# Where the taps of a 31-tap convolution are put in VectorE's queue

## The chip, the cores and the metric

The kernel runs on one core of one Trainium2 chip. The time is that of the device for one execution, in microseconds (us). TensorE (PE) multiplies, VectorE (DVE), ScalarE (ACT) and GpSimd (POOL) work elementwise, SyncE (SP) issues most loads. Every engine runs its own queue in the order in which the program was built, and waits for the others by semaphores.

## The reference

One layer of an encoder on x of 1024 positions by 1024 channels, all in float32. Cut to the part that matters:

```python
h = rms_norm(x, norm_mix_g[l]) * (1.0 + sc1) + sh1
proj = jnp.einsum('bsd,de->bse', h, w_in[l])                 # 1024 -> 7 * 1024
b_s, c_s, v_s, v_c, gl_c, gate_br = jnp.split(proj, SPLITS[:-1], axis=-1)
y_a = b_s * causal_dwconv(c_s * v_s, conv_short_w[l])        # 3 taps
y_a = jnp.einsum('bsc,cd->bsd', y_a, w_short_out[l])
u = v_c * jax.nn.sigmoid(gl_c)
u = causal_dwconv(u, conv_conf_w[l]) + conv_conf_b[l]        # 31 taps
u = jax.nn.silu(layer_norm(u, conf_ln_g[l], conf_ln_b[l]))
y_b = jnp.einsum('bsc,cd->bsd', u, w_conf_out[l])
g_a, g_b = jnp.split(jax.nn.sigmoid(gate_br), 2, axis=-1)
mix = jnp.einsum('bsd,de->bse', g_a * y_a + g_b * y_b, w_o[l])
```

After it come a residual, a SwiGLU feed-forward layer with its own residual, and a last RMSNorm.

## The kernel before

Channels lie on the 128 partitions (`KC` = 8 blocks), positions along the free axis in two halves of `H` = 512. Float32 products are made of three matmuls: an operand is split into a high and a low part (`wh`, `wl` for weights: ACT casts `wh`, L214, and POOL subtracts to `wl`, L215; `th`, `tl` for activations), and high*high, high*low and low*high are summed in PSUM (`mm3`, L309, L310, L312).

The input projection's 56 column blocks are made after a short lead in 12 *duals* (`PAIRS`). A dual takes two pairs of column blocks and replaces eight block products by seven, in the manner of Strassen and Winograd. The products are named by `PRODUCTS = "1265734"` and run in that order, each in two halves, one for each pair (p = 0, 1). A half is 12 matmuls into one PSUM bank. Banks are added up in place: 1, 6, 7 and 4 all go to bank x of their pair, 2 to bank y, 5 and 3 to bank z. So 7 may start only when the sum of 6 has been read out of x, and 4 only when that of 7 has. POOL also makes the sums of weight blocks that the products need (L234, L236, L238, L255).

`win_evac` reads the banks. After 1, 6 and 5 ACT copies them out (L642, L657). After 2, 7 and 3 DVE reads them with one addition, `plus` (L602), and each such instruction is appended to the list `reads`: six in a dual, in the order 2p0, 2p1, 7p0, 7p1, 3p0, 3p1. After 4, kinds "u" and "g" take a sigmoid on ACT (L670), "p" and "q" a product on DVE (`minus_times`, L606). Kind "u" makes an input of the 31-tap convolution (`u[j]`, L648, L672), "p" that of the 3-tap convolution (`short_conv`, first ACT L593, then DVE L595), "q" multiplies its result (L652), "g" two gates, whose sigmoids (L654, L664) wait in the list `late` until the next copy of ACT.

The 31-tap convolutions of the eight blocks, `conv(j)`, run on DVE during the duals. One has two differences of even and odd positions (L711, L712, all in SBUF), one start (L725) and 46 taps (L720), each a multiply-add on 128x512 with its sum in one of two PSUM banks of their own (`ps2`). They are traced after all duals, and are bound to a place in DVE's queue by `tc.issue_after(ins)`: the scheduler that builds the queues may not put the instruction ahead of `ins`, but may put it later. Tap n of convolution j is bound to a reading by its share of all taps:

```python
with tc.issue_after(reads[(j * TAPS + n) * CONV_READS // (KC * TAPS)]):
```

with `CONV_READS` = 70 of the 72 readings, so some 5.3 taps to each reading. `add_conv(j)` stores the result from ACT's queue (L738) and adds it on POOL to `tot` (L741), the sum over channels that `ln_mean` multiplies by ones on PE after the first block of the next stage (`ya`, L752).

Of the kernel before, what the change touches and what calls it, by code (L numbers as in the profile page):

```python
# [43 lines left out]
KC = D // P  # L44
# [42 lines left out]
]  # L87


CONV_READS = 70  # L90

# [22 lines left out]
def block_kernel(ctx: ExitStack, tc: tile.TileContext, x0, xT, c, vecs, ada, w_first, w_plain, w_duals,  # L116
# [32 lines left out]
    def ps2_tile(name):  # L149
        return ps2p.tile([P, H], F32, tag="ps2", name=name)  # L150
# [33 lines left out]
    def col(base, k):  # L184
        return vec[:, base + k : base + k + 1]
# [17 lines left out]
    pool_los = []  # L203
# [247 lines left out]
    def uc_tile(name, n=T + CK - 1, dt=F32):  # L451
        return ucp.tile([P, T + CK - 1], dt, tag="uc", name=name)[:, :n]
# [33 lines left out]
    for k in range(0, KC, 2):  # L486
        t = uc_tile("x0", T)
# [111 lines left out]
    reads = []  # L599
# [102 lines left out]
    NE = (T + CK - 1) // 2  # L702
    TAPS = CK // 2 * 3 + 2

    def conv(j):
        eo = u[j].rearrange("p (n two) -> p n two", two=2)
        ev, od = eo[:, :, 0], eo[:, :, 1]
        diff = diffp.tile([P, T + CK - 1], F32, tag="diff", name="diff")
        d, e = diff[:, :NE], diff[:, NE : 2 * NE - 1]
        with tc.issue_after(reads[j * CONV_READS // KC]):  # L710
            nc.vector.tensor_tensor(d, ev, od, ALU.subtract)  # L711
            nc.vector.tensor_tensor(e, ev[:, 1:], od[:, : NE - 1], ALU.subtract)  # L712
        a0, a1 = ps2_tile("c0"), ps2_tile("c1")
        n = 0

        def tap(out, src, s, wt, acc):
            nonlocal n
            n += 1
            with tc.issue_after(reads[(j * TAPS + n) * CONV_READS // (KC * TAPS)]):
                tap.ins = nc.vector.scalar_tensor_tensor(  # L720
                    out=out, in0=src[:, s : s + H], scalar=wt, in1=acc, op0=ALU.mult, op1=ALU.add
                ).ins

        with tc.issue_after(reads[j * CONV_READS // KC]):
            nc.vector.tensor_scalar(a0, od[:, :H], wsum[:, j : j + 1], col(V_CB, j), ALU.mult, ALU.add)  # L725
        for s in range(1, CK // 2 + 1):
            last = s == CK // 2
            tap(a0, od, s, col(V_CW + 2 * s * KC, j) if last else wsum[:, s * KC + j : s * KC + j + 1], a0)
        for s in range(CK // 2):
            tap(eo[:, :H, 1] if s == CK // 2 - 1 else a1, e, s, col(V_CW + (2 * s + 1) * KC, j), a1 if s else a0)  # L730
        for s in range(CK // 2 + 1):
            tap(eo[:, :H, 0] if s == CK // 2 else a0, d, s, col(V_CW + 2 * s * KC, j), a0)

    def add_conv(j):

        hi, lo = pool_los[min((j + 1) * CONV_READS * 7 // (6 * KC) + 5, 7 * n_duals + 1)]
        with tc.issue_after(hi):
            nc.scalar.dma_start(cv_dram[j], u[j][:, :T])  # L738
        with tc.issue_after(lo):
            for h in range(2):  # L740
                nc.gpsimd.tensor_tensor(tot[h], tot[h], u[j][:, halves[h]], ALU.add)  # L741
# [37 lines left out]
    n_duals = len(PAIRS) // 2  # L779
# [36 lines left out]
    for j in range(KC):  # L816
        conv(j)
        add_conv(j)
# [297 lines left out]
    n = 2 * GROUP * P  # L1116
# [184 lines left out]
```

## Time and profile before

| what | us |
|---|---|
| median of 3 runs | 1491.02 |
| lowest, highest run | 1489.75, 1492.7 |
| the profiled execution's own time | 1494.91 |
| its span, first to last instruction | 1493.1 |
| PE busy in the span | 1476.5 |
| DVE busy | 1207.1 |
| ACT busy, POOL busy | 597.6, 560.7 |
| the 232 taps with a difference as input (L720), one | 0.750 |

The duals run from 113.2 to 573.5 us of the span. In rows of the timeline the first number is the start, the second the time taken (all of a run of equal instructions together, with their count at the end), then engine, line, operation and out<-in with buffer numbers left out; in brackets the idle time before it and what ended it. In rows of the windows each engine has its busy time and number of instructions.

### The profile page before, as it was taken

What the parts mean: (1) busy time and instruction counts of PE and PEld (TensorE: products, weight loads), DVE (VectorE), ACT (ScalarE), POOL (GpSimd) and SP (SyncE); (2) the same over time, 40 slices, a digit from 0 to 9 for tenths busy, and PEclk for the clock granted to TensorE, in tenths of its full rate; (3) what the DMA queues carried; (4) which work ended last, traced back from release to release, by engine and by line L of the source; (5) the groups of instructions that cost most, each with busy time, mean ns of one, the idle gap of its engine ahead of it and who ended that gap; (6) DMA issues with size and microseconds to landing.
All of it is one profiled execution on the core that took longest, in us unless ns stands there. A gap on an engine that the chain in (4) does not pass through costs nothing.

```text
span 1493.1 us, 17891 instructions
## 1 busy us (share of the span) xinstructions
PE 1476.5 (99%) x6539; PEld 1211.6 (81%) x6539; DVE 1207.1 (81%) x1582; ACT 597.6 (40%) x854; POOL 560.7 (38%) x467
## 2 busy tenths in 40 slices
PE   9999999999999999999999999999999999999997
PEld 6788877888888887888788887888888888888887
DVE  6898899999899999758876699777777765677755
ACT  4753333333333344235335375444435443222235
POOL 0037768788788774410121001010111016545005
PEclk9999999999999999999999999999999999999999
DMA  8522213222223258456764425555555449998403
GB/s 332 215 78 71 99 57 128 71 85 99 85 71 99 59 210 317 147 184 225 254 205 159 159 87 195 185 183 180 176 177 171 152 152 371 351 310 261 137 29 113
DMA packets 83994, 247.79 MB, mean 166 GB/s; under 512 B 9665, under 2 KB 11841, under 8 KB 83906
## 3 DMA queue, kind: packets, MB, share of 16 engines
q1 hardware_dynamic: 43072, 138.43, 27.8%
q0 software_dynamic: 36944, 95.44, 19.4%
q10 hardware_dynamic: 3890, 12.78, 2.2%
q8 instruction: 51, 0.84, 0.2%
q14 instruction: 37, 0.30, 0.1%
HBM read 184.22 MB, written 62.39 MB: 165 GB/s over the span
## 4 chain that ended last, share of the span: by engine, by line
PE 47%; DVE 3%; issue 1%; POOL 0%; ACT 0%; DMA 0%; POOLq 0%; DVEq 0%; ACTq 0%
PE x L312 7%; PE x L309 7%; PE x L310 7%; PE z L312 4%; PE z L309 4%; PE z L310 4%; PE y L312 3%; PE y L310 3%; PE y L309 3%; PE mix L309 2%; PE mix L310 2%; PE mix L312 2%; PE yb L309 1%; PE yb L312 1%; PE yb L310 1%
## 5 line engine op out<-in xcount | busy, mean ns | idle before, releaser
L214 ACT CAST wh<-raw 128x1024 fp32r<-128x1024 f32 (+2 forms) x257 | 259.1, 1009 | 465.0 <-PE x L310 117.3
L215 POOL TENSOR_TENSOR wl<-raw,wh 128x1024 fp32r<-128x1024 f32 x92 | 238.8, 2602 | 114.2 <-ACT wh L214 105.7
L215 DVE TENSOR_TENSOR wl<-raw,wh 128x1024 fp32r<-128x1024 f32 (+2 forms) x165 | 188.2, 1141 | 43.5 <-ACT wh L214 41.2
L720 DVE SCALAR_TENSOR_TENSOR c<-diff,vec,c 128x512 f32<-128x512 f32 x232 | 172.2, 750 | 4.0
L1017 POOL DMA_DIRECT2D hid<-stage x71 | 37.8, 533 | 346.2 <-DVE stage L349 340.2
L309 PE MATMUL x<-th,wh 128*128 128x512 f32 x336 | 131.1, 390 | 2.4 <-DVE sig L602 1.3
L312 PE MATMUL x<-th,wl 128*128 128x512 f32 x336 | 130.7, 389 | 0.0
L310 PE MATMUL x<-tl,wh 128*128 128x512 f32 x336 | 130.7, 389 | 0.0
L720 DVE SCALAR_TENSOR_TENSOR c<-u,wsum,c 128x512 f32<-128x512 f32 x112 | 84.0, 750 | 2.1
L309 PEld LDWEIGHTS x<-th,wh 128*128 128x128 f32 x336 | 63.1, 188 | 16.8 <-DVE sig L602 1.7
L312 PEld LDWEIGHTS x<-th,wl 128*128 128x128 f32 x336 | 63.1, 188 | 13.0
L310 PEld LDWEIGHTS x<-tl,wh 128*128 128x128 f32 x336 | 63.1, 188 | 13.0
L309 PE MATMUL x<-t2h,wh 128*128 128x512 f32 x184 | 71.7, 390 | 1.6 <-ACT wh L214 1.2
L310 PE MATMUL x<-t2l,wh 128*128 128x512 f32 x184 | 71.5, 389 | 0.0
L312 PE MATMUL x<-t2h,wl 128*128 128x512 f32 x184 | 71.4, 390 | 0.1
L348 ACT CAST stage<-g 128x512 fp32r<-128x512 f32 x62 | 38.3, 621 | 79.8 <-DVE g L1006 39.8
L234 POOL TENSOR_TENSOR raw<-raw 128x1024 f32<-128x1024 f32 x12 | 29.7, 2478 | 96.8 <-DVE wl L215 94.8
L309 PE MATMUL z<-th,wh 128*128 128x512 f32 x168 | 65.4, 389 | 0.0
L310 PE MATMUL z<-tl,wh 128*128 128x512 f32 x168 | 65.4, 389 | 0.0
L312 PE MATMUL z<-th,wl 128*128 128x512 f32 x168 | 65.4, 389 | 0.0
L349 DVE TENSOR_TENSOR stage<-g,stage 128x512 fp32r<-128x512 f32 x62 | 42.3, 688 | 27.2 <-ACT stage L348 27.2
L1043 POOL DMA_DIRECT2D th<-hid x71 | 38.1, 536 | 47.9 <-PE x L312 27.3
(836 smaller groups left out, 4097.3 us busy)
## 6 DMA issues: line engine op xcount, KB each, us to landing
hid<-stage POOLq DMA_DIRECT2D x71, 512.0 KB, 4.6
raw<-in_w_fi SPq DMA_DIRECT2D x51, 512.0 KB, 4.0
raw<-in_w_duals SPq DMA_DIRECT2D x48, 512.0 KB, 3.5
th<-hid POOLq DMA_DIRECT2D x71, 256.0 KB, 5.7
tl<-hid POOLq DMA_DIRECT2D x71, 256.0 KB, 5.7
ada<-in_ada SPq DMA_DIRECT2D x24, 512.0 KB, 6.3
raw<-in_ada SPq DMA_DIRECT2D x24, 512.0 KB, 4.4
raw<-in_w_fo SPq DMA_DIRECT2D x24, 384.0 KB, 5.8
```

The source lines that it names most:

```text
L214: hi = nc.scalar.copy(wh, raw)
L215: lo = lo_engine.tensor_tensor(wl, raw, f32(wh), ALU.subtract)
L234: eng.tensor_tensor(a["s1"], a["21"], a["22"], ALU.add)
L309: nc.tensor.matmul(ps, wh, xh, start=first, stop=False, skip_group_check=again)
L310: nc.tensor.matmul(ps, wh, xl, start=False, stop=False, skip_group_check=again)
L312: mm3.ins = nc.tensor.matmul(ps, wl, xh, start=False, stop=last, skip_group_check=again).ins
L348: t_split.act = nc.scalar.copy(hi, src).ins
L349: t_split.ins = nc.vector.tensor_tensor(lo, src, f32(hi), ALU.subtract).ins
L720: tap.ins = nc.vector.scalar_tensor_tensor(out=out, in0=src[:, s : s + H], scalar=wt, in1=acc, op0=ALU.mult, op1=ALU.add).ins
L1017: nc.gpsimd.dma_start(hid_dram[key], s)
L1043: nc.gpsimd.dma_start(t, hid_dram[key][:, s])
```

## The change

The place in `reads` is no longer found by the share of readings but by the share of time. A dual has 14 halves. The readings become due at the ends of halves 3, 4, 9, 10, 11 and 12 of 14 (`READS_AT`), and a convolution's taps are spread evenly over 11.75 duals: a tap that is due at time t, counted in duals, is bound to the last reading that lies before t. The readings are unevenly placed (five halves between 2p1 and 7p0, and five from 3p1 to 2p0 of the next dual, one between the others), so more taps are bound to 2p1 and 3p1 and fewer to the other four. The store and the sum of a convolution are bound to the weight splits of the same share of time as before, but for rounding.

```diff
-CONV_READS = 70
+CONV_DUALS = 11.75
+READS_AT = [(2 * "1265734".index(m) + p + 1) / 14 for m in "273" for p in range(2)]
...
+    def read_at(t):
+        return reads[max([0] + [6 * d + i for d in range(n_duals) for i, at in enumerate(READS_AT) if d + at <= t])]
...
-        with tc.issue_after(reads[j * CONV_READS // KC]):
+        with tc.issue_after(read_at(j * CONV_DUALS / KC)):
             nc.vector.tensor_tensor(d, ev, od, ALU.subtract)
             nc.vector.tensor_tensor(e, ev[:, 1:], od[:, : NE - 1], ALU.subtract)
...
-            with tc.issue_after(reads[(j * TAPS + n) * CONV_READS // (KC * TAPS)]):
+            with tc.issue_after(read_at((j * TAPS + n) * CONV_DUALS / (KC * TAPS))):
                 tap.ins = nc.vector.scalar_tensor_tensor(
...
-        with tc.issue_after(reads[j * CONV_READS // KC]):
+        with tc.issue_after(read_at(j * CONV_DUALS / KC)):
             nc.vector.tensor_scalar(a0, od[:, :H], wsum[:, j : j + 1], col(V_CB, j), ALU.mult, ALU.add)
...
-        hi, lo = pool_los[min((j + 1) * CONV_READS * 7 // (6 * KC) + 5, 7 * n_duals + 1)]
+        hi, lo = pool_los[min(int((j + 1) * CONV_DUALS * 7 / KC) + 5, 7 * n_duals + 1)]
```

## The prediction

> **What bounds the kernel now.** I read the page first, then the windows of PE dual by dual, then the timeline where a dual was longer, then DVE's and POOL's queues ahead of that place. Below, product names are those of `PRODUCTS`; 7p0 is the first half of product 7 (pair 0), 7p1 the second. Lines are those of the kernel before.
>
> ```profile
> span 1493.1 us, 17891 instructions
> PE 1476.5 (99%) x6539; PEld 1211.6 (81%) x6539; DVE 1207.1 (81%) x1582; ACT 597.6 (40%) x854; POOL 560.7 (38%) x467
> ```
>
> PE is busy for all but 16.6 us, so an edit of DVE's order can only win where PE waits for DVE. The windows cut the twelve duals:
>
> ```profile
> core 0: us, PE busy (x) PEld busy (x) DVE busy (x) ACT busy (x) POOL busy (x), PEclk, DMA share, GB/s
> 113.20:151.30 38.10, 38.10 (x170) 31.54 (x169) 33.25 (x42) 14.91 (x20) 29.44 (x15) 1.00 0.21 70
> 151.30:189.40 38.10, 38.10 (x170) 31.55 (x169) 32.63 (x37) 12.68 (x17) 28.62 (x11) 1.00 0.28 97
> 189.40:230.80 41.40, 38.97 (x170) 31.30 (x169) 40.68 (x49) 12.21 (x16) 29.68 (x14) 1.00 0.17 51
> ...
> 535.40:573.50 38.10, 38.10 (x170) 31.54 (x169) 37.42 (x50) 22.40 (x36) 21.23 (x9) 1.00 0.79 290
> ```
>
> From 230.8 to 573.5 nine duals take 342.7, so 38.08 each and 2.72 for each of its 14 halves. Only dual 2 is longer: 41.40, or 3.3 us lost. DVE is full there (40.68) and has 5 us to spare in each of duals 0 and 1. The timeline names the three waits in dual 2:
>
> ```profile
> 212.08 0.68 DVE L602 TENSOR_TENSOR sig<-y,sig 128x512 f32<-128x512 f32 x1
> 212.68 3.12 DVE L720 SCALAR_TENSOR_TENSOR c<-diff,vec,c 128x512 f32<-128x512 f32 x4
> ```
> ```profile
> 212.79 0.63 ACT L654 ACTIVATE sig<-sig 128x512 f32<-128x512 f32 x1 [9.04 <-DVE sig L602]
> 213.33 1.03 ACT L214 CAST wh<-raw 128x1024 fp32r<-128x1024 f32 x1
> 214.27 0.58 ACT L642 COPY sig<-x 128x512 f32<-128x512 f32 x1
> ```
> ```profile
> 214.90 0.50 PE L309 MATMUL x<-th,wh 128*128 128x512 f32 x1 [0.89 <-ACT sig L642]
> ```
> ```profile
> 222.84 0.69 DVE L602 TENSOR_TENSOR z<-x,z 128x512 f32<-128x512 f32 x1
> ```
> ```profile
> 227.19 0.68 DVE L602 TENSOR_TENSOR sig<-x,sig 128x512 f32<-128x512 f32 x1
> ```
> ```profile
> 227.92 0.50 PE L309 MATMUL x<-th,wh 128*128 128x512 f32 x1 [1.31 <-DVE sig L602]
> ```
>
> First, DVE's reading of 2p1 at 212.08 is 11.8 us behind the end of that half (189.4 + 4 x 2.72 = 200.3). ACT's gate sigmoid waits 9.04 us for it, and behind it in ACT's queue stands the copy of bank x, which 7p1 needs. Then 4p0 and 4p1 wait for the readings of 7p0 and 7p1, which end at 223.53 and 227.87. Without any wait these three halves would start at 189.37 + 9, 12 and 13 x 2.72: 213.85, 222.01 and 224.73.
>
> **The change part by part.** Built, both programs hold the same instructions. PE's order is the same; ACT, POOL and SP exchange a few neighbours (the stores of conv 3 and 7, conv 3's sums in `tot`, two loads after the duals), at places where their queues have idle time. So only DVE's order counts. Taps between readings, before and after: after 2p1 of dual 0, 9 and 15; after 2p1 of dual 1, 9 and 12, and with them the set-up of conv 1 (L725, L711, L712), which before stood after 7p0 and around 3p0; before 2p0 of dual 2, 7 and 6; between 2p1 and 7p0 of dual 2, 13 and 12; between 7p0 and 7p1, 2 and 1. The end of conv 7 moves from behind the last splits of q to ahead of them.
>
> ```profile
> 137.96 0.69 DVE L602 TENSOR_TENSOR z<-x,z 128x512 f32<-128x512 f32 x1 [2.59 <-PE x L312]
> ```
> ```profile
> 176.04 0.69 DVE L602 TENSOR_TENSOR z<-x,z 128x512 f32<-128x512 f32 x1 [5.01 <-PE x L312]
> ```
> ```profile
> 182.02 2.47 DVE L711 TENSOR_TENSOR diff<-u 128x527 f32<-128x527 f32 x1
> 184.41 2.88 DVE L606 SCALAR_TENSOR_TENSOR p<-z,p 128x512 f32<-128x512 f32 x1
> 187.21 2.90 DVE L712 TENSOR_TENSOR diff<-u 128x526 f32<-128x526 f32 x1
> 190.04 0.74 DVE L720 SCALAR_TENSOR_TENSOR c<-u,wsum,c 128x512 f32<-128x512 f32 x1
> ```
> ```profile
> 181.51 2.42 POOL L215 TENSOR_TENSOR wl<-raw,wh 128x1024 fp32r<-128x1024 f32 x1
> 184.00 2.74 POOL L238 TENSOR_TENSOR raw<-raw 128x1024 f32<-128x1024 f32 x1
> 186.70 2.85 POOL L215 TENSOR_TENSOR wl<-raw,wh 128x1024 fp32r<-128x1024 f32 x1
> ```
>
> The four taps at 212.68 take 3.12 and one alone 0.74 (row 190.04), so one more costs 0.79. The other rows give the price of an operation whose operands all lie in SBUF: L711 ends 0.56 after POOL's row (183.93), L606 0.55 after the next (186.74), L712 0.56 after the third. It waits out POOL's running instruction and then takes 0.55; where POOL pauses it takes 0.7 (row 465.82 below).
>
> Dual 0: six taps are 4.8 us against 2.59 idle, so 7p0 is read 2.1 us later. It may be: it is free at 137.7 and 4p0 needs it at 145.9. Nothing up to dual 1 gives that back; POOL's waits make it 2.6.
>
> Dual 1: three more taps 2.4, L725 0.7, L711 0.6 (POOL's row ends as it comes) and L712 2.8 (behind the next row), less 5.01 idle, plus the 2.6: 7p0 is read 4 us later, still 3 us before 4p0 needs it. Behind it, one tap fewer (-0.8), and L711 (182.02 to 184.41, 2.4) and L712 (187.21 to 190.04, 2.8) are gone: DVE is 2 us ahead at 3p1. One tap fewer before 2p0 makes 2.8; one lock that L648 and L595 then meet later or earlier is worth up to 2.9 either way, and I take 3.3, since the walk through those rows has L648 wait 1 us where it waited 2.2.
>
> Dual 2: 2p1 is read 3.3 us earlier. The first wait (1.05) goes. 7p0 is read 4.1 earlier (a tap fewer) and ends at 219.4, against 222.01; 7p1 4.9 earlier, at 223.0 against 224.73. So all three waits go, with 1.7 us to spare: **-3.3**. Bounds: 0 (the locks eat it) and -3.3 (PE has no more to give there). What is late next is 2p0 of dual 3, which only frees a bank that is wanted a dual later.
>
> The end of the duals:
>
> ```profile
> 583.33 2.52 POOL L741 TENSOR_TENSOR tot<-tot,u 128x512 f32<-128x512 f32 x2 [5.65 <-DVE u L720]
> ```
> ```profile
> 584.15 0.39 PE L312 MATMUL ya<-q71h,wl 128*128 128x512 f32 x1
> 584.67 2.36 PE L752 MATMUL mu<-tot,ones 128*128 128x512 f32 x4
> ```
>
> The matmul of the mean starts 0.52 after the one before it, where matmuls follow each other every 0.227 (2.72 by 12): 0.29 lost. The second sum ends at 585.85, and its matmul cannot start before that; I take 0.5 for both. With conv 7 done four or five taps (3 to 4 us) earlier both go: **-0.5**, between -0.5 and 0.
>
> Duals 8 to 11 are the other side:
>
> ```profile
> 454.23 2.92 POOL L238 TENSOR_TENSOR raw<-raw 128x1024 f32<-128x1024 f32 x1
> 457.11 2.85 POOL L215 TENSOR_TENSOR wl<-raw,wh 128x1024 fp32r<-128x1024 f32 x1
> 460.05 2.41 POOL L255 TENSOR_TENSOR raw<-raw 128x1024 f32<-128x1024 f32 x1
> ```
> ```profile
> 460.91 0.68 DVE L606 SCALAR_TENSOR_TENSOR p<-x,p 128x512 f32<-128x512 f32 x1
> ```
> ```profile
> 465.82 0.69 DVE L711 TENSOR_TENSOR diff<-u 128x527 f32<-128x527 f32 x1
> 466.44 3.42 DVE L595 SCALAR_TENSOR_TENSOR sc<-p,vec,sc 128x1024 f32<-128x1024 f32 x1
> 469.78 1.79 DVE L712 TENSOR_TENSOR diff<-u 128x526 f32<-128x526 f32 x1
> ```
> ```profile
> 461.62 1.16 ACT L593 ACTIVATE sc<-p,vec 128x1024 f32<-128x1024 f32 x1 [1.26 <-DVE p L606]
> 462.68 0.57 ACT L642 COPY p<-x 128x512 f32<-128x512 f32 x1
> ```
> ```profile
> 529.35 0.68 DVE L602 TENSOR_TENSOR sig<-x,sig 128x512 f32<-128x512 f32 x1
> ```
> ```profile
> 567.87 0.68 DVE L602 TENSOR_TENSOR sig<-x,sig 128x512 f32<-128x512 f32 x1
> ```
>
> The set-up of conv 6 (L711, L712), here 0.69 and 1.79 us long, moves to between 3p0 and 3p1 of dual 8, where POOL's rows touch. Each operation in SBUF then waits for one of them: L711 ends at 454.7, L652 at 457.6, L712 at 460.6, 3p1's reading at 461.2, the first L606 at 463.5; then the next L606, three taps, and the L606 of 460.91 comes at 467.0. ACT's L593 holds the copy of bank x until 469.4; PE needs that for 6p0 of dual 9 at 459.25 + 4 x 2.72 = 470.1. No wait, by 0.7. DVE stays about 2.8 us later, less a few taps: 7p1 of dual 10 ends at 532.8 where 4p1 wants it at 497.33 + 13 x 2.72 = 532.7; 7p1 of dual 11 ends at 570.6, wanted at 570.8. I put **+0.4** for these, between 0 (no gap of PE lies there that could go) and +3, one POOL row.
>
> Sum: -3.3 - 0.5 + 0.4 = -3.4. The profiled execution took 1494.91, which becomes 1491.5; it lies 3.9 above the median of the three runs. PE's work is the same in them, so I take the difference off the median: 1491.02 - 3.4 = **1487.6 us**.
>
> **Rivals.** (A) My forecast, 1487.2 to 1488.0. (B) The waits go in part, or come back in part: locks in duals 1 and 2 leave 1 to 2 us of the 3.3, or duals 10 and 11 pay 1 to 3: 1488.2 to 1490.2. For it speak margins of 0.7, -0.1 and 0.2 us; against it that a wait of PE in dual 10 also gives DVE time for dual 11, so it is paid once. (C) Slower: POOL's lock in dual 8. If L606 (467.0 by my walk) meets three more POOL rows, 8.7 us, ACT releases the bank at 478.1 and PE waits 8.0 in dual 9: 1491.0 - 3.8 + 8.0 = 1495.2. It decides from 4.5 us behind my walk (the gain is eaten), and makes it slower by 0.2% from 7.5. Against it: only four operations there lie wholly in SBUF (L711, L652, L712, the first L606), and I have each waiting already. The Trainium skill ("SBUF — State Buffer", Who interferes with whom) speaks for this rival: a VectorE instruction with two SBUF inputs and a GpSimd instruction that reads SBUF exclude each other for the whole instruction, so moving such operations into POOL's dense stretch costs. The trace agrees (2.47 beside POOL, 0.69 without). (D) The change does not do what it says: the taps only set a lower bound on DVE's order, and the lateness in dual 2 comes from locks that stay: only the mean's wait goes, 1490.5.
>
> **How the numbers follow.** A 0.56, B 0.26, C 0.12, D 0.06. About 0.2% (3.0 us, a border at 1488.0) is what a measurement of this kernel tells from no change. A is faster, B and D within it, C slower: 0.56, 0.32, 0.12. The range leaves C out and takes A, B and D with the scatter of the runs (1.3 us below their median): 1486.2 to 1491.0.
>
> **What would show it.** Right: in the windows dual 2 is 38.1 long; no row of PE in it has an idle mark; DVE's idle before 7p0 of duals 0 and 1 is gone; L741's wait for `u` (5.65) is gone. Wrong: a PE row with an idle mark in dual 2, 9, 10 or 11, or ACT's L593 in dual 8 after 468.4 on the time scale of before.

## The result, and the profile after

| kernel | median, us | lowest to highest | runs |
|---|---|---|---|
| before, beside the changed kernel | 1491.11 | 1489.75 to 1493.18 | 7 |
| changed | 1498.32 | 1494.59 to 1500.08 | 7 |

The ratio is 1.0038 (95% interval 1.0024 to 1.0052): slower, where 1487.6 us was forecast. The profiled execution took 1495.21 us. The page of the changed kernel, span and busy time of each engine:

```profile
span 1493.4 us, 17886 instructions
PE 1473.7 (99%) x6539; PEld 1209.9 (81%) x6539; DVE 1213.2 (81%) x1582; ACT 597.8 (40%) x854; POOL 555.9 (37%) x467
```

The span is 0.3 us longer than before's 1493.1, but the two do not begin alike. PE's first rows of before, then of the changed kernel (start, time taken, and a count of matmuls at the end):

```profile
8.06 6.47 PE L476 MATMUL clock<-ones 128*128 128x128 f32 x32
...
20.68 2.84 PE L305 MATMUL lead<-x,raw 128*128 128x512 f32 x6 [0.41 <-ACT x L392]
```
```profile
6.26 3.84 PE L478 MATMUL clock<-ones 128*128 128x128 f32 x32
...
17.07 6.28 PE L307 MATMUL lead<-x,raw 128*128 128x512 f32 x14 [0.41 <-ACT x L394]
```

The same 32 matmuls take 3.84 us in place of 6.47, and the lead comes 3.6 us earlier. The traces' records of the granted clock say why: full clock begins 4.4 us after the first instruction here, 13.6 us after it in before. Over the fourteen traces of this document it begins at 4.4 to 5.1 us in four and at 12.2 to 14.1 us in ten, and all fourteen kernels open alike. So the difference is taken to belong to the execution and not to the change, though no kernel was traced with both beginnings. From the start of dual 0 (113.2 before, 109.6 after) to the last matmul the changed kernel is 3.9 us slower. The windows of PE cut at its own duals (busy time and instructions of each engine, then the granted clock):

```profile
core 0: us, PE busy (x) PEld busy (x) DVE busy (x) ACT busy (x) POOL busy (x), PEclk, DMA share, GB/s
109.60:147.70 38.10, 38.10 (x169) 31.55 (x169) 35.62 (x43) 13.76 (x19) 29.44 (x15) 1.00 0.22 70
147.70:185.80 38.10, 38.10 (x169) 31.54 (x168) 37.85 (x49) 13.68 (x18) 27.24 (x11) 1.00 0.29 97
185.80:223.90 38.10, 38.10 (x170) 31.56 (x169) 37.74 (x51) 12.42 (x16) 32.14 (x14) 1.00 0.22 70
...
452.40:492.00 39.60, 38.35 (x169) 31.42 (x168) 38.93 (x49) 11.94 (x15) 30.17 (x14) 1.00 0.28 94
492.00:538.00 46.00, 40.39 (x170) 32.48 (x169) 45.36 (x49) 12.22 (x16) 33.90 (x17) 0.93 0.22 69
```

Dual 2 is 38.1 where it was 41.4. Two new places are long: dual 9 with 39.6 and dual 10 with 46.0, the only one whose clock was not 1.00 throughout. By the starts of PE's matmuls, to the hundredth: dual 2 -3.33, dual 9 +1.59, dual 10 +7.85. The waits of PE name what ended them (us in total, times, longest):

```profile
PE x L311 <- DVE sig L604: 5.6, 1, 5.6
PE x L311 <- ACT p L644: 1.3, 1, 1.3
...
PE yb L311 <- DVE gb L866: 0.9, 2, 0.6
```

**Dual 9.** From the timeline, POOL, DVE, ACT, PE:

```profile
442.14 2.40 POOL L238 TENSOR_TENSOR raw<-raw 128x1024 f32<-128x1024 f32 x1
```
```profile
442.32 2.77 DVE L608 SCALAR_TENSOR_TENSOR sc<-z,sc 128x512 f32<-128x512 f32 x1
...
449.10 1.30 DVE L717 TENSOR_TENSOR diff<-u 128x527 f32<-128x527 f32 x1
450.32 2.89 DVE L654 TENSOR_TENSOR sc<-v,sc 128x512 f32<-128x512 f32 x1
453.13 2.90 DVE L718 TENSOR_TENSOR diff<-u 128x526 f32<-128x526 f32 x1
...
462.26 0.68 DVE L608 SCALAR_TENSOR_TENSOR p<-x,p 128x512 f32<-128x512 f32 x1
```
```profile
462.98 1.15 ACT L595 ACTIVATE sc<-p,vec 128x1024 f32<-128x1024 f32 x1 [9.51 <-DVE p L608]
```
```profile
464.65 0.50 PE L311 MATMUL x<-t2h,wh 128*128 128x512 f32 x1 [1.25 <-ACT p L644]
```

L717, L654 and L718 wait out POOL's rows, as the prediction walked through (lines are 2 higher now, 6 from the convolutions on). But the walk started the set-up where DVE had stood in the kernel before, and DVE came to it 2.5 us later in the dual: it came to the reading 3p0 (448.50) 34.2 us after dual 8's start, and in before 31.8 after it. Of this, 1.45 stood already at the reading 7p0, behind 12 taps since 2p1 in place of 11, and 1.0 came with the product at 442.32: it asked 0.18 us after POOL's row had begun and took 2.77, where it had taken 1.75. The last product ends at 462.94, 10.6 us after dual 9's start; the walk had 8.4 (467.68 less 459.25), and 0.7 to spare.

**Dual 10.** POOL's queue, then DVE's, then PE's, all from the timeline:

```profile
518.52 1.28 POOL L830 DMA_DIRECT2D ga<-gate_a  x2
519.80 2.44 POOL L217 TENSOR_TENSOR wl<-raw,wh 128x1024 fp32r<-128x1024 f32 x1
522.17 1.32 POOL L747 TENSOR_TENSOR tot<-tot,u 128x512 f32<-128x512 f32 x1
523.42 2.44 POOL L236 TENSOR_TENSOR raw<-raw 128x1024 f32<-128x1024 f32 x1
525.79 1.31 POOL L747 TENSOR_TENSOR tot<-tot,u 128x512 f32<-128x512 f32 x1
527.04 2.37 POOL L238 TENSOR_TENSOR raw<-raw 128x1024 f32<-128x1024 f32 x1
529.36 2.34 POOL L217 TENSOR_TENSOR wl<-raw,wh 128x1024 fp32r<-128x1024 f32 x1
531.78 2.70 POOL L240 TENSOR_TENSOR raw<-raw 128x1024 f32<-128x1024 f32 x1
```
```profile
525.46 6.80 DVE L608 SCALAR_TENSOR_TENSOR sc<-z,sc 128x512 f32<-128x512 f32 x1
...
532.84 0.68 DVE L604 TENSOR_TENSOR sig<-x,sig 128x512 f32<-128x512 f32 x1
```
```profile
527.58 0.39 PE L314 MATMUL x<-th,wl 128*128 128x512 f32 x1
533.58 0.80 PE L311 MATMUL x<-th,wh 128*128 128x512 f32 x1 [5.61 <-DVE sig L604]
534.17 0.63 PE L312 MATMUL x<-tl,wh 128*128 128x512 f32 x1
534.60 0.63 PE L314 MATMUL x<-th,wl 128*128 128x512 f32 x1
```

The product asked at 525.46, 0.4 us before the end of L236. It did not get in there, nor at the end of the sum L747, nor at that of L238; each next row of POOL follows without a gap. It got in after L217 (531.70), where L240 begins 0.08 us later, and ended 0.56 behind that, as always. So it got in at the fourth end that it met instead of the first. Behind it stands the reading of 7p1 (532.84), and PE waits for that. Then the matmuls come every 0.427 us (534.17 to 534.60) in place of 0.227: the clock had fallen. The windows of that stretch, with the granted clock behind the engines:

```profile
528.00:530.00 2.00, 0.00 (x0) 0.00 (x0) 2.00 (x1) 0.00 (x0) 2.00 (x2) 1.00 0.00 0
530.00:532.00 2.00, 0.00 (x0) 0.00 (x0) 2.00 (x1) 0.00 (x0) 1.92 (x2) 0.51 0.00 0
```

So dual 10's 7.85 are 5.77 of waiting (527.58 to 533.58, less one spacing), 1.65 of half clock (533.58 to dual 11's first matmul at 537.95 is 4.37 for 12 matmuls that take 2.72 else) and 0.4 of small gaps.

**The end of the duals.** POOL and PE, from the timeline:

```profile
581.62 2.55 POOL L747 TENSOR_TENSOR tot<-tot,u 128x512 f32<-128x512 f32 x2
```
```profile
586.69 0.39 PE L314 MATMUL ya<-q71h,wl 128*128 128x512 f32 x1
586.91 1.88 PE L758 MATMUL mu<-tot,ones 128*128 128x512 f32 x4
```

L747's 5.65 us of waiting are gone, and the matmul of the mean follows 0.22 after the one before. The stages from there to the variance are 0.7 us shorter. One more difference, -1.3, stands in PE's wait in `yb` (0.9 against 2.2). It runs from 0.2 to 1.8 in the traces below without regard to the change.

### The profile page after: what moved, and what is told of

Its sections match the earlier page's. It is cut to its first block, busy times and chain, and to the rows that moved or that the text cites. A ratio compares the mean times of both kernels' runs of the same rounds, so it can differ in the third digit from the quotient of the medians.

```text
span 1493.4 us, 17886 instructions
## 1 busy us (share of the span) xinstructions
PE 1473.7 (99%) x6539; PEld 1209.9 (81%) x6539; DVE 1213.2 (81%) x1582; ACT 597.8 (40%) x854; POOL 555.9 (37%) x467
## 4 chain that ended last, share of the span: by engine, by line
PE 47%; DVE 3%; issue 1%; POOL 0%; ACT 0%; DMA 0%; POOLq 0%; DVEq 0%; ACTq 0%
PE x L314 7%; PE x L311 7%; PE x L312 7%; PE z L311 4%; PE z L312 4%; PE z L314 4%; PE y L311 3%; PE y L314 3%; PE y L312 3%; PE mix L312 2%; PE mix L311 2%; PE mix L314 2%; PE yb L311 1%; PE yb L312 1%; PE yb L314 1%; DVE wl L217 1%
## 5 line engine op out<-in xcount | busy, mean ns | idle before, releaser
L217 POOL TENSOR_TENSOR wl<-raw,wh 128x1024 fp32r<-128x1024 f32 x92 | 238.0, 2592 | 128.4 <-ACT wh L216 119.6
L217 DVE TENSOR_TENSOR wl<-raw,wh 128x1024 fp32r<-128x1024 f32 (+2 forms) x165 | 188.2, 1141 | 46.5 <-ACT wh L216 44.6
L236 POOL TENSOR_TENSOR raw<-raw 128x1024 f32<-128x1024 f32 x12 | 29.6, 2468 | 94.9 <-DVE wl L217 91.3
L1049 POOL DMA_DIRECT2D th<-hid x71 | 38.1, 536 | 50.8 <-PE x L314 31.0
```

The lines of the kernel that those rows point to most:

```text
L217: lo = lo_engine.tensor_tensor(wl, raw, f32(wh), ALU.subtract)
L236: eng.tensor_tensor(a["s1"], a["21"], a["22"], ALU.add)
L1049: nc.gpsimd.dma_start(t, hid_dram[key][:, s])
```

## The experiments

All are made from the changed kernel unless said otherwise. Durations of duals are PE's, start to start; "the product" is `sc<-z,sc` of dual 10. The letters of theories in the expectations are those of the experiments, not the prediction's rivals. Ratios are to the kernel before on the same chip, with 95% intervals.

**1. The changed kernel again.**

> The changed kernel once more, beside the kernel before. Theory A (place and lock): the change gains 3.3 us in dual 2 and loses 1.6 in dual 9 and 7.9 in dual 10, the same in every execution, so the duals from the start of dual 0 to the end of dual 11 take 466.4 us again (460.3 before), and the two kernels differ by about +4 us when they start alike; executions fall into two groups some 3.6 us apart for both kernels, by when dual 0 begins (109.6 or 113.2). Theory B (the start): the stage lengths of the duals vary from execution to execution, and the median's +7 us is chance; then the twelve duals take another time than 466.4 and the ratio to the kernel before falls within 1.000 to 1.002.

Median 1499.0 (6 runs), ratio 1.004 (1.0026 to 1.0055). Dual 9 took 39.63, dual 10 45.52, the product 6.82. It is no accident of one execution; theory B falls. The profiled runs of both, 1495.21 and 1494.99, have the early lead (17.1). The thirteen runs of this kernel, seven and six, fall in groups, 1494.6 to 1495.2 and 1498.3 to 1500.1; that the upper one is the late start is likely (the close variant of experiment 5, lead at 20.8, took 1498.75), but no run of that group has a trace.

**2 and 3. Convolutions 0 to 4, or 3 to 7, by time, the others by readings as before.**

```diff
+    def at(j, n):
+        if j in TIMED:                     # (0, 1, 2, 3, 4), then (3, 4, 5, 6, 7)
+            return read_at((j * TAPS + n) * CONV_DUALS / (KC * TAPS))
+        return reads[(j * TAPS + n) * CONV_READS // (KC * TAPS)]
...
-            with tc.issue_after(read_at((j * TAPS + n) * CONV_DUALS / (KC * TAPS))):
+            with tc.issue_after(at(j, n)):
```

> Only convolutions 0 to 4 are placed by time, 5 to 7 by readings as before: VectorE's order is that of the changed kernel up to dual 6 and that of the kernel before from the readings of dual 7 on. Theory A (the loss is made in duals 8 to 10 by the set-up of convolution 6): dual 2 at 38.1, no dual longer than 38.3; 3.3 us less than before, or 4.6 with the wait of 1.3 us at the second half of yb, if that goes too: about 1487. Theory C (the taps drawn ahead fill VectorE and are paid later, wherever they are placed): a wait in duals 8 to 11 stays and the time is at or above that of the kernel before, 1491 to 1498.

Median 1489.79 (11 runs), ratio 0.9985 (0.9976 to 0.9995); all twelve duals 38.08. About 1487 was expected: the ratio is worth 2.2 us, less than the 3.3 that dual 2 gains, though its interval reaches 3.6.

> The other half: convolutions 0 to 2 placed by readings as before, 3 to 7 by time. Theory A: dual 2 is 41.4 long again, dual 9 39.7 and dual 10 45.9 as in the changed kernel; 1.6 + 7.9 = 9.5 us more than before less 0.5 to 1.8 at the mean and yb, about 1499 where the kernel before takes 1491. Theory C: duals 9 and 10 are long only because duals 0 to 2 drew taps ahead; then they are 38.1 here and the time is that of the kernel before.

Median 1501.98 (6 runs), ratio 1.0065 (1.0052 to 1.0078); dual 2 41.31, dual 9 39.63, dual 10 45.96. So the gain belongs to the early convolutions and the loss to the late ones, and dual by dual they add up to those of the changed kernel; theory C falls.

**4. The sums of conv 6 six weight splits later**, so that they don't stand in dual 10's stretch.

```diff
-        hi, lo = pool_los[min(int((j + 1) * CONV_DUALS * 7 / KC) + 5, 7 * n_duals + 1)]
+        hi, lo = pool_los[min(int((j + 1) * CONV_DUALS * 7 / KC) + 5 + 6 * (j == 6), 7 * n_duals + 1)]
```

> The changed kernel with one edit: the two GpSimd additions of convolution 6 to the channel sums, and its store, are bound six weight splits later, behind dual 10's sums of weight blocks. In dual 10 GpSimd's instructions then stand in the order of dual 4, where each of two sums has a pause of 0.08 us ahead of it. Theory A (VectorE's product waits while GpSimd's instructions follow each other without a pause): the product that took 6.80 us takes 0.6 to 2.9, dual 10 is 38.1 to 39 long, dual 9 stays 39.7, and the time falls by 6 to 8 us, to about 1490. Theory C (VectorE is too late in dual 10 by its taps alone): dual 10 stays over 41 and the time over 1494.

Median 1491.53 (12 runs), ratio 0.9993 (0.9985 to 1.0002). Dual 9 stayed at 39.63, dual 10 fell to 39.37 with the clock at 1.00, the product to 2.44. That shows that the lost ends cost 6 to 7 us. It does not show why they were lost: without the sums POOL also paused 0.23 us ahead of L236, to wait for a load.

**5 and 6. A short and a long pause on DVE ahead of the product** (two memsets of 30 or 248 elements), so that it asks at another point of POOL's row.

```diff
-                    minus_times(sc[j + 1][:, halves[1]], e["z"], sc[j + 1][:, halves[1]])
+                    with ExitStack() as order:
+                        for _ in range(2 if j == 6 else 0):
+                            order.enter_context(tc.issue_after(reads[-1]))
+                            pause = nc.vector.memset(pad[:, :30], 0.0).ins      # or :248
+                            order.enter_context(tc.issue_after(pause))
+                        minus_times(sc[j + 1][:, halves[1]], e["z"], sc[j + 1][:, halves[1]])
```

> The changed kernel with two small VectorE memsets (128x30 each, 0.08 us) ahead of the product in dual 10 that took 6.80 us. There it was issued 0.39 us before the end of a GpSimd instruction and let three more go ahead. Theory D (a request that comes in the last 0.4 us of a GpSimd instruction loses, and goes on losing until GpSimd pauses): it now comes 0.15 to 0.3 us before that end and still takes 6.3 to 6.8 us; dual 10 stays at 45 to 46. Theory E (it loses to the channel sums' instructions whenever it comes): the same here. Theory F (pure chance at each boundary): some other length, 0.6 to 4.

One run, 1498.75; the product came 0.31 us before an end, lost, and took 6.71; dual 10 45.15.

> The same with two longer memsets (128x248), so that the product comes about 0.4 to 0.7 us later, after the end of that GpSimd instruction and some 1 us before the end of the next, the first addition of the channel sums. Theory D: it gets in at that next end, takes 1.3 to 2 us in place of 6.8, so that a pause makes the kernel faster: dual 10 falls to 38.1 to 39.5. Theory E: it still waits for both following instructions, 5.5 to 6.3 us, and dual 10 stays over 44. Theory F: 0.6 to 4 us.

One run, 1499.55; the product came 1.11 us before an end, lost it and one more and took 6.28; dual 10 45.96. Theory D, that an instruction loses if it comes in the last 0.4 us, falls. Theory F of these two expectations, chance at each end, falls with it: in both the product waited on to the same pause, behind the second weight split (L217 of the changed kernel). Theory E, that the channel sums behind it decide, still fits here.

**7. The set-up of conv 6 behind the last product of its block's pair in dual 8.**

```diff
-                    minus_times(e["b"][0], ps, e["b"][0])
+                    p_done[j] = minus_times(e["b"][0], ps, e["b"][0])
...
-        with tc.issue_after(read_at(j * CONV_DUALS / KC)):
+        with tc.issue_after(p_done[6] if j == 6 else read_at(j * CONV_DUALS / KC)):
             nc.vector.tensor_tensor(d, ev, od, ALU.subtract)
```

> The changed kernel with the two differences of convolution 6 bound behind the last product of pair p6 in dual 8, so out of the stretch between the readings of product 3. Theory A: ScalarE's 3-tap start and the bank copy behind it come 5 to 6 us earlier, dual 9 falls from 39.7 to 38.1. VectorE and GpSimd then meet in dual 10 at other phases: by theory D the product there takes 0.6 to 2.9 us unless it again comes in the last 0.4 us of a GpSimd instruction; dual 10 at 38.1 to 39.5, and the time near 1488 to 1490. Theory C (too many taps drawn ahead): dual 9 or 10 stays over 39.5.

Median 1488.99 (10 runs), ratio 0.9978 (0.9964 to 0.9991), all duals 38.08. So the set-up in POOL's dense stretch is the cause of dual 9's wait. In dual 10 the product still asked in L236 with a sum L747 behind it, and got in at once, in 1.87 us: theory E falls as well. POOL had paused 0.91 us ahead of L236.

**8 and 9. One small addition on DVE in dual 10** (128x30, both inputs in SBUF), behind tap 8 or tap 10 of conv 7.

```diff
+            if j == 7 and n == 8:                  # or 10
+                with tc.issue_after(tap.ins):
+                    nc.vector.tensor_tensor(pad[:, 60:90], pad[:, :30], pad[:, 30:60], ALU.add)
```

> Edit: the changed kernel with one more instruction on VectorE in dual 10, an addition of 128x30 with both inputs in SBUF, behind the eighth tap of conv 7, so some 21 us into POOL's dense stretch, about 4.5 us before the product sc<-z,sc; it asks while POOL's L217 of 2.4 us runs, 1.1 us before that row's end. It writes scratch only. Theory F: the product loses because POOL had run at least three instructions, some 6 us or more, one right behind the other, with no instruction of VectorE in between; in all nine traces an instruction that asked after a shorter stretch got in at the first end, at most 6.03 us into the stretch, and the five losers asked behind 6.04 us or more. Then the small addition, if it gets in at the end of L217 or of the sum L747 (1.1 to 2.5 us), breaks the stretch, and the product, which comes 1 to 2.5 us later, gets in at the first end: under 2.6 us in place of 6.80, dual 10 in 39 to 41.5 us in place of 45.9, no half clock, the whole some 5 us less than the changed kernel. Theory E (the product loses wherever the channel sums L747 stand in POOL's queue behind it, however POOL ran before): the product waits on until POOL pauses at the end of the next L217, 4 to 6 us, and dual 10 stays over 44. If the addition itself loses several ends in a row, F holds with an earlier border, and the product comes late all the same.

> Edit: as before, but the small addition stands behind the tenth tap of conv 7, so that it asks while the sum L747 (1.3 us) runs, 0.8 us before its end, in a stretch of POOL that is then longer by that row. Theory F: by that time POOL has run over 7 us without a break, and the addition itself loses several ends in a row (over 3 us, up to 9 until POOL pauses); the product follows it at once and dual 10 stays over 44 us. If the addition gets in at the end of L747 (1.2 us), length of the stretch alone is not what decides, and the product, about 1.2 us later than before, again tells: under 2.6 us (a break helps) or 4 to 6 us (theory E).

The addition itself waited, in the timeline of the first:

```profile
524.45 9.82 DVE L732 TENSOR_TENSOR fill<-fill 128x30 f32<-128x30 f32 x1
```

It asked 0.38 us before the end of the first weight split (L217 of the changed kernel) behind the two issues of `ga`, and lost five ends, until POOL paused. POOL's unbroken stretch was then 5.7 us old, behind a pause of 7.86, and not 21 us as the expectation has it. In the second kernel it took 8.24. Dual 10 took 49.71 and 47.55, the runs 1504.35 and 1501.40. So a small addition waits like the large product, and the shut stretch begins no later than that L217. Theory F (from experiment 8 on: the length of POOL's unbroken stretch) survives with an earlier border. But laid side by side the traces held a plainer mark: where an end was lost, POOL had not paused since it issued the loads of `ga` (L830); where VectorE got in, POOL had paused after them (before: 0.43 us, experiments 2, 4 and 7: 0.42, 0.23 and 0.91). That is theory G. The pause of the kernel before is in its timeline, POOL's row of that place, and the product behind it:

```profile
523.57 1.82 POOL L741 TENSOR_TENSOR tot<-tot,u 128x512 f32<-128x512 f32 x1 [0.43 <-DVE u L720]
```
```profile
527.13 1.65 DVE L606 SCALAR_TENSOR_TENSOR sc<-z,sc 128x512 f32<-128x512 f32 x1
```

The product asked during L234 there and got in at its end (528.23), though POOL's next row followed without a gap. POOL waited ahead of L741 for the last tap of conv 6. In the changed kernel that tap is done earlier, the sum (L747, 522.17) follows at once, and the opening is gone.

**10. The first two loads of `ga` issued by SyncE.**

```diff
-            nc.gpsimd.dma_start(ga, gate_dram["a", j][:, halves[h]])
+            (nc.gpsimd if j else nc.sync).dma_start(ga, gate_dram["a", j][:, halves[h]])
```

> Edit: the changed kernel with the first two loads of a gate (L830, ga) issued by SyncE instead of GpSimd; they stood in POOL's queue in dual 10, right ahead of the stretch in which the product loses. The order of DVE, ACT and PE is as in the changed kernel, POOL's too but for these two issues. Theory G, formed on the seven traces with a loser: after POOL has issued a DMA itself, it keeps VectorE's two-input instructions out at every end of an instruction until it pauses; in all seven nothing of POOL's paused between the two issues and the lost ends, and in the other four traces it paused there (0.2 to 0.9 us) and VectorE got in at the first end. G expects: the product at most 2.6 us long, dual 10 between 38.1 and 39.5 us in place of 45.9, no half clock, dual 9 still 39.6; the whole some 7 us below the changed kernel, ratio to the kernel before 0.998 to 1.0005. Theory F (the length of POOL's unbroken stretch alone, 6 us or more): POOL's L217, L217, L747, L236 still follow each other without a pause, so the product still loses, dual 10 stays over 44 us and the ratio over 1.002. Theory E (the channel sums behind it): the same as F.

The timeline, POOL and then DVE:

```profile
518.54 4.79 POOL L217 TENSOR_TENSOR wl<-raw,wh 128x1024 fp32r<-128x1024 f32 x2 [7.87 <-ACT wh L216]
523.27 1.29 POOL L747 TENSOR_TENSOR tot<-tot,u 128x512 f32<-128x512 f32 x1
524.52 2.41 POOL L236 TENSOR_TENSOR raw<-raw 128x1024 f32<-128x1024 f32 x1
526.88 1.31 POOL L747 TENSOR_TENSOR tot<-tot,u 128x512 f32<-128x512 f32 x1
528.12 2.88 POOL L238 TENSOR_TENSOR raw<-raw 128x1024 f32<-128x1024 f32 x1
```
```profile
527.83 0.91 DVE L608 SCALAR_TENSOR_TENSOR sc<-z,sc 128x512 f32<-128x512 f32 x1
```

POOL runs the same five instructions without a pause for 9.65 us, and the product gets in at the first end that it meets, 0.35 us after it asked. Dual 10 takes 38.10, dual 9 39.63. Median 1490.18 (12 runs), ratio 0.9987 (0.9975 to 1.0). Theories E and F wanted over 44 us.

**11. A load of 128x30 issued by GpSimd late in dual 4**, where VectorE had got in in every other trace.

```diff
+                    if m == "1" and len(made) == 6:        # made: the sums of L238
+                        with tc.issue_after(made[-1]):
+                            nc.gpsimd.dma_start(pad[:, :30], w_conf[0][:, :30])
```

> Edit: the changed kernel with one more load issued by GpSimd, 128x30 into scratch, behind the second weight sum (L238) near the end of dual 4, where L238, L217, L747, L240, L747 and L217 follow one another without a pause and where VectorE's product p<-z,p got in at the end of L747 (1.63 us) in the changed kernel. Theory G: behind that issue the product loses at each end until POOL pauses, behind the second L217: 5 to 9 us instead of 1.63, and PE waits for it in dual 4 or 5 (2 to 7 us, half clock if over 3). Theories F and E: the product gets in at the first end as before (0.6 to 2.6 us), duals 4 and 5 stay at 38.1 us; a load of its own changes nothing. Dual 9 and 10 as in the changed kernel in either case, unless the waits move them.

POOL and DVE, from the timeline (lines are 2 to 5 higher in this kernel than in the changed one):

```profile
295.86 0.73 POOL L257 DMA_DIRECT2D fill<-in_w_conf  x1
296.60 2.42 POOL L219 TENSOR_TENSOR wl<-raw,wh 128x1024 fp32r<-128x1024 f32 x1
298.97 1.29 POOL L752 TENSOR_TENSOR tot<-tot,u 128x512 f32<-128x512 f32 x1
300.22 2.39 POOL L242 TENSOR_TENSOR raw<-raw 128x1024 f32<-128x1024 f32 x1
302.57 1.28 POOL L752 TENSOR_TENSOR tot<-tot,u 128x512 f32<-128x512 f32 x1
303.81 2.39 POOL L219 TENSOR_TENSOR wl<-raw,wh 128x1024 fp32r<-128x1024 f32 x1
306.28 2.74 POOL L262 TENSOR_TENSOR raw<-raw 128x1024 f32<-128x1024 f32 x1
```
```profile
298.27 8.49 DVE L613 SCALAR_TENSOR_TENSOR p<-z,p 128x512 f32<-128x512 f32 x1
```

The product of dual 4, 1.63 us in the changed kernel, takes 8.49: it loses four ends and gets in at 306.20, where POOL pauses 0.08 us. Dual 5 pays 1.3, where 2 to 7 were expected, and the lateness goes on to dual 9 (42.41); in dual 10 (45.48) the product loses three ends again. One run, 1502.36. With experiment 10 this shows theory G from both sides: a load issued by GpSimd shuts VectorE's instructions with two inputs in SBUF out until GpSimd pauses. It is the issue and not the transfer: here the load had landed at 297.94, before the product asked, and in the changed kernel both loads of `ga` had landed by 523.57, and the product, asking at 525.46, still lost three ends.

**12. Both remedies**, the edits of 7 and 10.

> Edit: the changed kernel with both remedies: the set-up of conv 6 behind the last product of its block's pair in dual 8, and the first two gate loads issued by SyncE. Theory G with the reading of dual 9 (the set-up in POOL's dense stretch makes VectorE late there): all twelve duals 38.08 us, no instruction of VectorE over 3 us by POOL's lock, no half clock; the whole some 1 us or less below the kernel with the set-up alone, since in that one the product in dual 10 got in by luck of a pause; ratio 0.9965 to 0.9985. If either reading is wrong, dual 9 or dual 10 is over 38.5 us.

Median 1488.06 (12 runs), ratio 0.9971 (0.996 to 0.9982), all duals 38.08, the product 1.48: the lowest ratio measured here. That it beats experiment 7 is not shown; the intervals overlap.

## Why the prediction was wrong

- **Dual 2, -3.3: right.** It lost 3.33 us, and no row of PE in it has an idle mark. The readings of 7p0 and 7p1 begin at 212.37 and 215.36, so they end 27.3 and 30.2 us after the dual's start, where 30.0 and 33.6 were forecast: there was more to spare than thought. Experiments 2 and 3 give the gain to the early convolutions.
- **Duals 0 and 1: right.** DVE's idle there was filled (35.62 and 37.85 busy against 33.25 and 32.63), and PE lost nothing.
- **The mean's wait, -0.5: right in kind**, and 0.7 from the mean to the variance, a little beyond its bound.
- **Duals 8 to 11, +0.4: this is the step that failed**, by 9.0 us: 1.6 in dual 9 and 7.8 in dual 10 in its place. Of the marks that were to show it wrong, two came: PE idle in 9 and 10, and L593 of dual 8 late (462.98 is 469.9 on before's scale, with 3.6 for the start and 3.3 for dual 2; the bound was 468.4).
  - In dual 9 the mechanism was the one walked through, and the size was off: the walk let DVE come to the set-up as in the kernel before, and it came 2.5 us later, 1.45 by the taps moved ahead of 7p0 and 1.0 by the product that met a row of POOL.
  - In dual 10 the bound "+3, one POOL row" was wrong in kind. It took from the rows of dual 1 that an instruction waits out the running row of POOL and then gets in. That held wherever POOL had issued no load since its last pause. Here it had, and one row became four. A gap of 6 us then halved the clock, a price that no term had.
- **Rival C** (slower at 0.12) named the lock and "three more POOL rows", with 8.0 us for it. The price was near, the place wrong: it was not in dual 8 but in dual 10, where no operation had been moved into the stretch, and the order of POOL's queue is the same there. What the change took away was a wait: POOL's 0.43 us for the last tap of conv 6, ahead of the sum, which had let VectorE in. The prediction named POOL's wait at the end of the duals as a gain and did not ask what the same wait did in dual 10.
- **The Trainium skill** ("SBUF — State Buffer", Who interferes with whom) says that whoever issues first holds the shared ports for the whole instruction and the other fully blocks. That agrees with each single row here (0.56 us after POOL's end). It speaks of one instruction; that several rows of GpSimd which begin after VectorE has asked can go first is not in what it says, and the 6.80 and 9.82 us decide.
- **The reference to the median**: the difference was taken off the median of three, 1491.02. From dual 0 on, the traces say +3.9; the ratio says +5.7, and the medians lie 7.2 apart. The rest fits other shares of early and late starts, but that is argued, not shown.

## What to carry to other kernels

Before work is moved on VectorE, look at what GpSimd's queue does around each instruction with two inputs in SBUF, not only whether it is busy: a load that GpSimd issues itself, followed by dense elementwise work, can hold VectorE for all of that work, and another queue for the load cured it here. A wait for a shared port is not bounded by one row of the other engine unless the trace shows it in that very stretch, so price a late operation by the whole stretch up to the next pause. And a wait of TensorE of several us has a second price, the halved clock behind it.

## What the hardware showed that was not expected

- In eight traces (the changed kernel, experiments 1, 3, 5, 6, 8, 9 and 11) instructions of VectorE with two inputs in SBUF lost two to five ends of GpSimd's rows in a row, always in a stretch without a pause behind a load that GpSimd had issued, and always up to a pause as short as 0.08 us. Even 128x30 elements waited 9.82 us. Elsewhere they got in at the first end that they met, in half of some 570 such waits in the duals of the fourteen traces with GpSimd's next row touching. Why a pause frees them is open.
- The clock halved when TensorE had been idle some 2.1 us (last matmul done at 527.97, half clock from about 530.0), for 6.8 us. In experiment 11 an idle time of 2.58 us did it for 3.4 us, in experiment 5 the clock stood at 1.00 for over 4 us of idle time before it fell, and 1.25 us in dual 9 did nothing. The Trainium skill ("TensorE: Matmul & The Clock Gate", Part 1) gives a free-running window of about 3.4 us, idle for at least one to fall to half. One and two windows fit the two lengths (three the 10.2 us of experiment 8), and a window that runs by itself fits the scatter; that it must be idle throughout does not fit, since TensorE had been idle for less than 3.4 us when the clock fell in the changed kernel and in experiment 11.
- The beginning differs from trace to trace: the lead started at 17.1 us in the four of the fourteen whose full clock began at 4.4 to 5.1 us, and at 20.0 to 20.9 in the ten where it began at 12.2 to 14.1, a difference as large as the effect that was to be measured.
